# State-space layer: the product of the scores between two row tiles with weighted x as three fp32r passes over high and low parts instead of one plain fp32 matmul, with one buffer for the far sum

## The chip, the core and the metric

The kernel runs on one core of one Trainium2 chip. The metric is the device time of one execution in microseconds; the time quoted is the median of several runs. Besides the runs, one execution is profiled. TensorE (PE in the profile, with its weight loads as PEld), VectorE (DVE), ScalarE (ACT), GpSimd (POOL) and SyncE (SP, which here issues nearly all transfers) work from queues of their own and wait for each other through semaphores.

## The reference

A decoder trunk of two layers on 256 tokens of width 2048: an attention layer (MLA) and a state-space layer (SSM), each followed by a squared-ReLU MLP, all in fp32. What matters here is the scan of the SSM layer, which with 256 tokens is one chunk. It has 8 groups of 8 heads of 64 channels, and states of 128.

```
cum = jnp.cumsum(la_c, axis=1)
decay = jnp.exp(jnp.where(tril[None, :, :, None, None], diff, -jnp.inf))
cb = jnp.einsum('blgn,bsgn->blsg', c_c, b_c)
y_diag = jnp.einsum('blsgh,bsghp->blghp', cb[..., None] * decay, x_c)
```

So each head's output is a lower-triangular 256 by 256 matrix (scores `cb` times decay) times x.

## The kernel before

Tokens lie in two row tiles of 128. The triangle is cut into two tiles on the diagonal, which are computed head by head, and one full tile that leads from the first 128 tokens to the last 128. The decay in that tile splits into a factor of the source row and a factor of the target row. So the tile is done for a whole group at once: x of the first row tile is multiplied by the source factor (`edge[:, 0]`, on GpSimd, line 1257), the scores between the row tiles (`cb[g][:, P:256]`, 128x128) are multiplied with it on TensorE (128x512, line 1261), and VectorE multiplies the result by the target factor into `far[g]` (line 1263). GpSimd later adds `far[g]` to the second row tile (line 1314), and VectorE adds the diagonal products (line 1320).

Almost all of TensorE's work is large matrix products in fp32r. Every operand is held as a high part (rounded to fp32r by a ScalarE copy) and a low part (the rest, a VectorE subtraction), and a product is three passes: high times high, low times high, high times low. Weights arrive in units of 128x1024: SP loads one (`wraw`, line 85, six buffers), ScalarE writes its high part (`wh`, line 102), VectorE its low part (`wl`, line 103), four buffers each, and TensorE uses it in twelve matmuls of 512 columns (lines 339, 340, 343). The product of line 1261 is not of this kind: both operands are plain fp32.

A block is a set of four keys, each of two such units; after each key `tick()` runs what has been put off with `later(n, ...)`, so a step put off by 0 comes one tick later and one put off by 1 two ticks later. TensorE's order is the order in which the program is written. For the other engines a scheduler sets the order; `behind("last")`, `behind("last_lo")` and `behind("last_load")` put an instruction behind the last `wh` copy on ScalarE, the last `wl` subtraction on VectorE, or the last weight load on SP.

`x_block(g)` computes x of group g. Its convolution reads three shifted copies of x from DRAM (`taps`, two transfers of 768 KB, line 1229) and the convolution weights (`cw`, 128x2560, one buffer, line 1213), multiplies them (lines 1234 and 1235), sums them (1239) and applies SiLU (1244, 1247). Then `ahead` starts the heads of the group and the product described above. `head` loads a row of cumulative sums for each head (`cm`, line 1287) and builds the decay (ACT lines 1291 and 1292, DVE line 1294). Scratch tiles of 128x512 come from a pool of seven (`s2`).

Of the kernel before, what the change touches and what calls it, by code (L numbers as in the profile page):

```python
# [20 lines left out]
F32 = mybir.dt.float32  # L21
F32R = mybir.dt.float32r
I32 = mybir.dt.int32
AF = mybir.ActivationFunctionType
ALU = mybir.AluOpType
# [3 lines left out]
P = 128  # L29
# [185 lines left out]
class Trunk:  # L215
# [851 lines left out]
    def ssm_body(self, sp, dp, gain):  # L1067
        nc, d, cst = self.nc, self.d, self.cst
# [9 lines left out]
        cb = [None] * GROUPS  # L1078
# [4 lines left out]
        far = [None] * GROUPS  # L1083
# [18 lines left out]
        def behind(what):  # L1102
            return self.tc.issue_after(getattr(self.flow, what).ins)
# [88 lines left out]
        def cb_group(g):  # L1192
            B, C = fm["B", g // 4][:, g % 4], fm["C", g // 4][:, g % 4]
            b = self.bank(early[0])
            nc.tensor.matmul(b[:, 0:256], B[:, 0:P], C, start=True, stop=True)
            nc.tensor.matmul(b[:, 256:384], B[:, P:256], C[:, P:256], start=True, stop=True)
            t = sp.tile([P, 384], F32, tag="cb", name=f"cb{g}", bufs=5)
            for o in (0, 256):
                nc.vector.scalar_tensor_tensor(t[:, o:o + P], b[:, o:o + P], 0.125, tri[:, 0:P], ALU.mult, ALU.mult)
            cb[g] = t  # L1200

            def far_part():
                with behind("last"):
                    nc.scalar.activation(t[:, P:256], b[:, P:256], AF.Copy, scale=0.125)

            self.later(0, far_part)

        def x_block(g):
            cw = []

            def weights():
                cw.append(sp.tile([P, 2560], F32, tag="cw", name=f"cw{g}", bufs=1))
                nc.sync.dma_start(cw[0], d["cwx"][g])

            self.later(3, weights)
            accs = self.block([("si", "x", g, q) for q in range(4)], xT)
            xt = sp.tile([P, 2, 512], F32, tag="xtm", name=f"xtm{g}", bufs=3)
            x = [xt[:, t] for t in range(2)]
            th = [None, None]
            for t in range(2):  # L1220
                nc.scalar.activation(x[t], accs[t], AF.Copy, scale=rs[t])
            nc.scalar.dma_start(xD[3:S + 3, g * 512:g * 512 + 512].rearrange("(t p) n -> p t n", t=2), xt)

            def shift():
                with behind("last_load"):
                    for t in range(2):
                        v = xD[t * P:t * P + P, g * 512:g * 512 + 512]
                        row = v.ap[0][0]
                        nc.sync.dma_start(taps[:, t], bass.AP(tensor=v.tensor, offset=v.offset, ap=[[row, P], [row, 3], [1, 512]]))

            def mult(t):
                flat = taps[:, t].rearrange("p i n -> p (i n)")
                with behind("last_lo"):
                    nc.vector.tensor_tensor(flat, flat, cw[0][:, :1536], ALU.mult)
                    nc.vector.tensor_tensor(x[t], x[t], cw[0][:, 1536:2048], ALU.mult)

            def total(t):
                for v in (taps[:, t, 2], taps[:, t, 1], taps[:, t, 0], cw[0][:, 2048:]):
                    nc.vector.tensor_tensor(x[t], x[t], v, ALU.add)

            def tanh(t):
                th[t] = self.scratch()
                with behind("last"):
                    nc.scalar.activation(th[t], x[t], AF.Tanh, scale=0.5)

            def silu(t):
                nc.vector.scalar_tensor_tensor(x[t], th[t], 1.0, x[t], ALU.add, ALU.mult)

            def ahead():
                xg[g] = x  # L1250
                dg = self.gain_tile(d["dsk"][g])
                for i in range(8):
                    hq.append((g, i, dg))
                heads_of = lambda v: v.rearrange("p (h f) -> p h f", h=8)
                spread = lambda v: v[:, 8 * g:8 * g + 8].unsqueeze(2).to_broadcast([P, 8, 64])
                xw = self.scratch()
                nc.gpsimd.tensor_tensor(heads_of(xw), heads_of(x[0]), spread(edge[:, 0]), ALU.mult)

                def across():
                    b = self.bank(False)  # L1260
                    nc.tensor.matmul(b, cb[g][:, P:256], xw, start=True, stop=True)
                    far[g] = sp.tile([P, 512], F32, tag="far", name=f"far{g}", bufs=2)
                    nc.vector.tensor_tensor(heads_of(far[g]), heads_of(b), spread(edge[:, 1]), ALU.mult)

                self.later(1, across)

            self.later(2, shift)
            if g >= 4:
                self.later(2, lambda: cb_group(g))
            self.later(4, lambda: (mult(0), mult(1)))  # L1270
            self.later(5, lambda: total(0))
            self.later(6, lambda: (tanh(0), total(1)))
            self.later(7, lambda: (silu(0), tanh(1), silu(1), ahead()))

        def pump():
# [88 lines left out]
        for step in SSM_ORDER:  # L1364
            kind, i = step[0], int(step[1])
# [242 lines left out]
```

## Time and profile before

| | before |
|---|---|
| runs | 2285.92 us median of 3 (2285.37 to 2287.04) |
| the profiled execution | 2286.35 us, of which the span is 2284.5 |
| TensorE / VectorE / ScalarE / GpSimd busy | 100% / 84% / 61% / 12% of the span |
| granted TensorE clock | 1.00 |
| SSM groups' product (line 1261) | 8 of them, at 1080.5 to 1502.6 us of the span |

Times in the profile are counted from the start of the span. A group row gives the line, engine, operation and tiles, then the number of instructions, their busy time in us and the mean of one in ns, then the idle time before them. A row of a timeline gives the start, the duration from first start to last end, and a count of equal instructions that follow each other; a bracket at its end is idle time before it and what ended that. TensorE's matmuls overlap, so their pace is read from starts. A plain fp32 matmul is recorded as two.

### The profile page before, as it was taken

Reading aid. Unit: us, or ns where it says so; the run is one execution under the profiler, and the core shown is the slowest. Engines: PE = TensorE matmul, PEld = TensorE weight load, DVE = VectorE, ACT = ScalarE, POOL = GpSimd, SP = SyncE. Lnnn points to the kernel's source line nnn. Section 1 sums busy time; section 2 is a strip of 40 time slices with the busy share of each in tenths; the row PEclk is TensorE's granted clock in tenths of the full one; section 3 lists DMA queues with packets and bytes.
Section 4 is the critical chain, followed back from the end, with each engine's and each line's share of the span. In section 5 each row is a group of like instructions: output and inputs, shape, how many; then the busy total and the mean of one; then the engine's idle time right before and its main releaser. Section 6 shows DMA issues by size and latency. Waiting matters only on the chain.

```text
span 2284.5 us, 30768 instructions
## 1 busy us (share of the span) xinstructions
PE 2278.1 (100%) x10929; PEld 1889.6 (83%) x10929; DVE 1915.9 (84%) x2318; ACT 1390.1 (61%) x1947; POOL 275.5 (12%) x315
## 2 busy tenths in 40 slices
PE   9999999999999999999999999999999999999999
PEld 7898888888888888888888888888888888888887
DVE  7786698999898897687899688676989889989985
ACT  7775576566666666564666555545666666666663
POOL 1440000000000000100133213121000000000000
PEclk9999999999999999999999999999999999999999
DMA  8545678888888878667888787767688888888874
GB/s 315 173 153 159 211 230 267 259 255 270 264 255 259 267 232 271 227 208 241 277 280 278 245 275 264 229 222 229 204 265 248 259 270 253 260 275 247 267 232 160
DMA packets 167706, 557.16 MB, mean 244 GB/s; under 512 B 19040, under 2 KB 28192, under 8 KB 166528
## 3 DMA queue, kind: packets, MB, share of 16 engines
q1 hardware_dynamic: 151264, 502.44, 66.2%
q0 software_dynamic: 13888, 48.49, 10.0%
q10 hardware_dynamic: 2400, 4.27, 0.5%
q8 instruction: 86, 1.41, 0.3%
q14 instruction: 68, 0.56, 0.1%
HBM read 529.65 MB, written 6.41 MB: 235 GB/s over the span
## 4 chain that ended last, share of the span: by engine, by line
PE 96%; DVE 1%; DMA 1%; ACT 1%; issue 1%; POOL 0%; SPq 0%; ACTq 0%; DVEq 0%
PE acc L339 13%; PE acc L340 13%; PE acc L343 13%; PE yp L618 9%; PE yp L617 9%; PE yp L616 9%; PE st L617 7%; PE st L618 7%; PE st L616 7%; DMA wraw<-mi 1%; PE sm L324 1%; DVE wl L103 1%; PE y L1309 1%; PE sm L322 1%; PE acc L616 1%; PE acc L618 1%
## 5 line engine op out<-in xcount | busy, mean ns | idle before, releaser
L102 ACT ACTIVATE wh<-wraw 128x1024 fp32r<-128x1024 f32 (+1 forms) x818 | 856.2, 1053 | 570.4 <-PE acc L340 268.9
L103 DVE TENSOR_TENSOR wl<-wraw,wh 128x1024 fp32r<-128x1024 f32 (+1 forms) x818 | 985.5, 1221 | 240.6 <-ACT wh L102 216.6
L616 PE MATMUL yp<-wh,k 128*128 128x512 f32 x896 | 349.2, 390 | 0.0
L618 PE MATMUL yp<-wh,k 128*128 128x512 f32 x896 | 348.8, 389 | 0.0
L617 PE MATMUL yp<-wl,k 128*128 128x512 f32 x896 | 348.6, 389 | 0.0
L339 PE MATMUL acc<-wh,xt 128*128 128x512 f32 x704 | 279.7, 397 | 0.4 <-ACT wh L102 0.4
L340 PE MATMUL acc<-wh,xt 128*128 128x512 f32 x704 | 274.9, 390 | 0.1
L102 ACT ACTIVATE wh<-wrx 128x1024 fp32r<-128x1024 f32 x168 | 177.8, 1058 | 153.4 <-PE yp L618 101.7
L103 DVE TENSOR_TENSOR wl<-wrx,wh 128x1024 fp32r<-128x1024 f32 x168 | 204.3, 1221 | 36.6 <-ACT wh L102 35.6
L618 PEld LDWEIGHTS yp<-wh,k 128*128 128x128 f32 x896 | 168.2, 188 | 35.1
L617 PEld LDWEIGHTS yp<-wl,k 128*128 128x128 f32 x896 | 168.2, 188 | 34.9
L616 PEld LDWEIGHTS yp<-wh,k 128*128 128x128 f32 x896 | 168.2, 188 | 34.8
L339 PE MATMUL acc<-wh,k 128*128 128x512 f32 x496 | 196.5, 396 | 0.0
L340 PE MATMUL acc<-wh,k 128*128 128x512 f32 x496 | 193.3, 390 | 0.0
L343 PE MATMUL acc<-wl,xt 128*128 128x512 f32 x704 | 188.3, 389 | 0.0
L616 PE MATMUL st<-wh,xt 128*128 128x512 f32 x448 | 177.7, 397 | 0.0
L618 PE MATMUL st<-wh,xt 128*128 128x512 f32 x448 | 174.9, 390 | 0.0
L617 PE MATMUL st<-wl,xt 128*128 128x512 f32 x448 | 174.7, 390 | 0.0
L339 PEld LDWEIGHTS acc<-wh,xt 128*128 128x128 f32 x704 | 132.7, 188 | 29.4 <-ACT wh L102 1.6
L340 PEld LDWEIGHTS acc<-wh,xt 128*128 128x128 f32 x704 | 132.5, 188 | 28.5 <-issue 1.2
L343 PEld LDWEIGHTS acc<-wl,xt 128*128 128x128 f32 x704 | 132.1, 188 | 27.7
L199 POOL DMA_DIRECT2D wrx<-mi x56 | 49.2, 878 | 720.6 <-DVE wl L103 524.5
(318 smaller groups left out, 3527.0 us busy)
## 6 DMA issues: line engine op xcount, KB each, us to landing
wraw<-mi SPq DMA_DIRECT2D x256, 512.0 KB, 5.5
wraw<-mo SPq DMA_DIRECT2D x256, 512.0 KB, 5.6
wraw<-si SPq DMA_DIRECT2D x160, 512.0 KB, 5.2
wraw<-so SPq DMA_DIRECT2D x64, 512.0 KB, 5.2
wrx<-mi SPq DMA_DIRECT2D x56, 512.0 KB, 5.4
wrx<-mi POOLq DMA_DIRECT2D x56, 512.0 KB, 7.8
wraw<-wo SPq DMA_DIRECT2D x32, 512.0 KB, 4.0
taps<-xD SPq DMA_DIRECT2D x16, 768.0 KB, 8.4
```

Of the source, the lines that this page charges most:

```text
L102: self.last = nc.scalar.activation(h[:, v], raw[:, v], AF.Copy)
L103: self.last_lo = nc.vector.tensor_tensor(lo[:, v], raw[:, v], h[:, v].bitcast(F32), ALU.subtract)
L199: nc.gpsimd.dma_start(st["b11"].tile, quarter(d, 1, 0), accum_op=ALU.add)
L322: self.nc.tensor.transpose(b.bitcast(F32R)[:, v], words[:, v], self.ident_r)
L324: self.nc.tensor.transpose(b[:, v], src[:, v], self.ident)
L339: nc.tensor.matmul(accs[t][:, :n], ah, wh[:, q, :], start=first and kt + q == 0, stop=False)
L340: nc.tensor.matmul(accs[t][:, :n], al, wh[:, q, :], start=False, stop=False)
L343: nc.tensor.matmul(accs[t][:, :n], lhs(kt + q, t)[0], wl[:, q, :], start=False, stop=en and q == nk - 1)
L616: nc.tensor.matmul(b, ah, wh, start=first and q == 0, stop=False)
L617: nc.tensor.matmul(b, ah, wl, start=False, stop=False)
L618: nc.tensor.matmul(b, al, wh, start=False, stop=last and q == 1)
L1309: nc.tensor.matmul(y[t][c, o], part(t)[:, c], xg[g][t][:, o], start=True, stop=True)
```

## The change

```
-                xw = self.scratch()
+                xw = cw[0][:, :512]
+                xh, xl = (self.s2.tile([P, 512], F32R, tag="s2", name=self.name("xw")) for _ in range(2))
+                fh = sp.tile([P, 2, P], F32R, tag="fh", name=f"fh{g}", bufs=1)
                 nc.gpsimd.tensor_tensor(heads_of(xw), heads_of(x[0]), spread(edge[:, 0]), ALU.mult)
+                with behind("last"):
+                    nc.scalar.activation(fh[:, 0], cb[g][:, P:256], AF.Copy)
+                with behind("last_lo"):
+                    nc.vector.tensor_tensor(fh[:, 1], cb[g][:, P:256], fh[:, 0].bitcast(F32), ALU.subtract)
+
+                def parts():
+                    with behind("last"):
+                        nc.scalar.activation(xh, xw, AF.Copy)
+                    with behind("last_lo"):
+                        nc.vector.tensor_tensor(xl, xw, xh.bitcast(F32), ALU.subtract)
+
+                self.later(0, parts)
 
                 def across():
                     b = self.bank(False)
-                    nc.tensor.matmul(b, cb[g][:, P:256], xw, start=True, stop=True)
-                    far[g] = sp.tile([P, 512], F32, tag="far", name=f"far{g}", bufs=2)
+                    for i, (a, w) in enumerate(((0, xh), (0, xl), (1, xh))):
+                        nc.tensor.matmul(b, fh[:, a], w, start=i == 0, stop=i == 2)
+                    far[g] = sp.tile([P, 512], F32, tag="far", name=f"far{g}", bufs=1)
                     nc.vector.tensor_tensor(heads_of(far[g]), heads_of(b), spread(edge[:, 1]), ALU.mult)
 
                 self.later(1, across)
```

The scores (`fh`) and weighted x (`xh`, `xl`) are split like other operands, and the product becomes three fp32r passes. The scores are split in `ahead` itself, weighted x one tick later, and the passes come another tick later, at the product's place. Weighted x in fp32 has no scratch tile of its own any more: it overwrites the first 512 columns of the group's convolution weights. The new tiles `xh` and `xl` come from the pool of scratch tiles. `far` has one buffer instead of two. Lines behind the edit are 15 higher in the changed kernel: 1294 is 1309, 1320 is 1335, 1287 is 1302, and 1263 is 1278 there; its product is line 1276.

The order on VectorE around the product of group 2, before. `wl` are low parts of weights, `mt` the decays of single heads, `xtm` is x (the L1320 rows add the diagonal products of group 1):

```order
L103 TENSOR_TENSOR wl_10830<-wraw_10727,wh_10829 128x1024
L1320 SCALAR_TENSOR_TENSOR xtm_9865<-xtm_9865,y_0_10690 128x512
L1320 SCALAR_TENSOR_TENSOR xtm_9865<-xtm_9865,y_1_10691 128x512
L103 TENSOR_TENSOR wl_10866<-wraw_10745,wh_10865 128x1024
L1294 SCALAR_TENSOR_TENSOR mt_10995<-mt_10995,dt,cb_9591 128x128 x2
```

The same place in the changed kernel. The row of line 1269 writes `xl` (named `xw` here, as `xh` is) from weighted x in `cw`:

```order
L103 TENSOR_TENSOR wl_10850<-wraw_10743,wh_10849 128x1024
L1335 SCALAR_TENSOR_TENSOR xtm_9869<-xtm_9869,y_0_10706 128x512
L1335 SCALAR_TENSOR_TENSOR xtm_9869<-xtm_9869,y_1_10707 128x512
L1269 TENSOR_TENSOR xw_10786<-cw_10325,xw_10785 128x512
L103 TENSOR_TENSOR wl_10888<-wraw_10761,wh_10887 128x1024
L103 TENSOR_TENSOR wl_10906<-wraw_10829,wh_10905 128x1024
```

The subtraction stands behind the two adds and ahead of the low parts of the next weight units.

The order on SP's queue at the load of group 2's convolution weights (`cw`), before. `wraw` are weight units, `cm` cumulative sums of heads, `taps` the shifted copies of x of group 2:

```order
L1213 DMA cw_10313<-cwx 128x2560
L85 DMA wraw_10391<-si 128x1024
L85 DMA wraw_10409<-si 128x1024
L85 DMA wraw_10439<-si 128x1024
L1287 DMA cm_10795<-cumD 128x256
L1287 DMA cm_10847<-cumD 128x256
L85 DMA wraw_10457<-si 128x1024
L1229 DMA taps<-xD 128x3x512 x2
```

The same stretch in the changed kernel:

```order
L1302 DMA cm_10815<-cumD 128x256
L85 DMA wraw_10405<-si 128x1024
L85 DMA wraw_10423<-si 128x1024
L85 DMA wraw_10455<-si 128x1024
L1302 DMA cm_10869<-cumD 128x256
L1213 DMA cw_10325<-cwx 128x2560
L85 DMA wraw_10473<-si 128x1024
L1229 DMA taps<-xD 128x3x512 x2
```

The load of `cw`, which needs the buffer that now holds weighted x of group 1, stands three weight units and two `cm` rows later, with one weight unit between it and `taps`.

On TensorE only the product itself differs: one row of line 1261 is now three of line 1276 at the same place.

## The prediction

> **What bounds the kernel now.** I read the page first, then the waits of TensorE over the whole run, then the busy time of the engines in stretches of the SSM layer, then the timelines around each of the eight products that change.
>
> ```profile
> span 2284.5 us, 30768 instructions
> PE 2278.1 (100%) x10929; PEld 1889.6 (83%) x10929; DVE 1915.9 (84%) x2318; ACT 1390.1 (61%) x1947; POOL 275.5 (12%) x315
> PE 96%; DVE 1%; DMA 1%; ACT 1%; issue 1%; POOL 0%; SPq 0%; ACTq 0%; DVEq 0%
> ```
>
> TensorE is busy for the whole span and is 96% of the chain that ended last. Its waits for other engines, line by line (total, times, longest), in the whole run:
>
> ```profile
> PE warmed L451 <- DVE warm L448: 1.4, 1, 1.4
> PE yp L939 <- ACT xt L944: 0.5, 1, 0.5
> PE yp L939 <- DVE qn L887: 0.4, 1, 0.4
> PE acc L339 <- ACT wh L102: 0.4, 1, 0.4
> ```
>
> That is 2.7 us in all, none of it in the SSM layer. So nothing can be gained but TensorE's own work, and any new wait of TensorE is added in full. The engine that is nearest to causing one is VectorE. Two stretches of the SSM layer (busy time of TensorE, weight load, VectorE, ScalarE, GpSimd, then granted clock, DMA share and GB/s):
>
> ```profile
> 1122.00:1131.00 9.00, 9.00 (x39) 7.11 (x38) 9.00 (x15) 7.09 (x14) 1.43 (x1) 1.00 1.01 386
> 1144.50:1177.60 33.10, 33.10 (x205) 27.11 (x204) 32.48 (x43) 18.54 (x35) 15.37 (x8) 1.00 0.78 256
> ```
>
> VectorE has no idle time in the first and 0.62 us of 33.1 in the second. Its queue runs behind there, and what is newly put into it comes out late. The first row also shows the DMA engines full at 386 GB/s.
>
> **What the change takes from TensorE.** One product and its neighbours on TensorE, for group 2 (start, duration, a count at the end):
>
> ```profile
> 1174.57 1.07 PE L343 MATMUL acc<-wl,xt 128*128 128x512 f32 x4
> 1175.48 1.02 PE L1261 MATMUL sm<-s,cb 128*128 128x512 f32 x2
> 1175.93 0.80 PE L339 MATMUL acc<-wh,xt 128*128 128x512 f32 x1
> 1176.57 0.40 PE L340 MATMUL acc<-wh,xt 128*128 128x512 f32 x1
> ```
>
> Durations overlap, so I go by starts. Four fp32r products take 1175.48 - 1174.57 = 0.91, 0.23 us each. From the start of the plain fp32 product (one instruction, recorded twice) to that of L340 are 1.09 us, of which one slot of 0.23 is the L339 between: the product costs 0.86. Three fp32r passes cost 3 x 0.23 = 0.68. The saving is 0.18 us, times 8 groups 1.4 us. It is on the path.
>
> **What it adds to the other engines.** Nearest rows (count, busy total, mean ns) for the four splits per group:
>
> ```profile
> L1235 DVE TENSOR_TENSOR xtm<-xtm,cw 128x512 f32<-128x512 f32 x16 | 10.9, 680 | 0.0
> L1199 DVE SCALAR_TENSOR_TENSOR cb<-sm,tri 128x128 f32<-128x128 f32 x12 | 2.9, 283 | 0.0
> L1244 ACT ACTIVATE s<-xtm 128x512 f32<-128x512 f32 x16 | 9.8, 625 | 17.8 <-DVE xtm L1239 17.7
> L1204 ACT ACTIVATE cb<-sm 128x128 f32<-128x128 f32 x6 | 1.6, 262 | 0.3 <-DVE cb L1199 0.3
> ```
>
> The high parts cost ScalarE 0.63 + 0.26 us, the low parts VectorE 0.68 + 0.28, per group. ScalarE has room (18.54 of 33.10) and its share counts as nothing. VectorE's share matters for when the low part of weighted x (`xl`) is ready, since the second of the three passes needs it. It waits for the multiply on GpSimd, the copy on ScalarE, and whatever stands ahead of it in VectorE's queue. The product's place on TensorE is fixed, between the same two units of weights as before, so I can set the two times against each other. In the new order `xl` stands in groups 1, 2, 3, 4 and 6 right behind the two L1320 adds. In groups 0, 5 and 7 the queue is short. The row on VectorE (for group 0 on GpSimd) that goes before `xl` in the new order, and the product, group by group (group 2's product is above):
>
> ```profile
> 1075.29 3.64 POOL L1257 TENSOR_TENSOR s<-xtm,edge 128x512 f32<-128x512 f32 x1 [119.67 <-PE acc L343]
> 1080.47 1.02 PE L1261 MATMUL sm<-s,cb 128*128 128x512 f32 x2
> 1127.10 1.27 DVE L1320 SCALAR_TENSOR_TENSOR xtm<-xtm,y 128x512 f32<-128x512 f32 x2
> 1128.10 1.02 PE L1261 MATMUL sm<-s,cb 128*128 128x512 f32 x2
> 1175.23 1.27 DVE L1320 SCALAR_TENSOR_TENSOR xtm<-xtm,y 128x512 f32<-128x512 f32 x2
> 1222.61 1.27 DVE L1320 SCALAR_TENSOR_TENSOR xtm<-xtm,y 128x512 f32<-128x512 f32 x2
> 1222.86 1.02 PE L1261 MATMUL sm<-s,cb 128*128 128x512 f32 x2
> 1269.71 1.27 DVE L1320 SCALAR_TENSOR_TENSOR xtm<-xtm,y 128x512 f32<-128x512 f32 x2
> 1270.92 1.02 PE L1261 MATMUL sm<-s,cb 128*128 128x512 f32 x2
> 1358.46 0.35 DVE L1294 SCALAR_TENSOR_TENSOR mt<-mt,dt,cb 128x128 f32<-128x128 f32 x1
> 1362.50 1.02 PE L1261 MATMUL sm<-s,cb 128*128 128x512 f32 x2
> 1409.33 1.27 DVE L1320 SCALAR_TENSOR_TENSOR xtm<-xtm,y 128x512 f32<-128x512 f32 x2
> 1410.56 1.02 PE L1261 MATMUL sm<-s,cb 128*128 128x512 f32 x2
> 1497.82 1.94 DVE L103 TENSOR_TENSOR wl<-wraw,wh 128x1024 fp32r<-128x1024 f32 x1
> 1502.14 1.02 PE L1261 MATMUL sm<-s,cb 128*128 128x512 f32 x2
> ```
>
> `xl` ends at the end of that row plus 0.28 (the other subtraction, queued a little earlier) plus 0.68, less two overlaps of 0.08, so plus 0.80. TensorE wants it at the product's start plus the 0.23 of the first pass. Group 1: 1128.37 + 0.80 = 1129.17 against 1128.33, a wait of 0.84. Group 2: 1177.30 against 1175.71, 1.59. Group 3: 1224.68 against 1223.09, 1.59. Group 4: 1271.78 against 1271.15, 0.63. Group 6: 1411.40 against 1410.79, 0.61. Group 0: GpSimd ends at 1078.93, copy and subtraction bring it to 1080.24 against 1080.70, no wait. Groups 5 and 7: 1359.6 against 1362.73 and 1500.6 against 1502.37, no wait. The sum is 5.3 us. Behind a waiting TensorE stand only its own next matmuls, which are the path.
>
> **What moves on SP's queue.** The weighted x now lies in `cw`, the buffer of the convolution weights. The load of the next group's `cw` must therefore wait until `xl` is written, and stands three weight loads later, just ahead of the `taps` loads. Before, for group 2 on SP, with median landing times (us, last column) of these transfers, then what ScalarE and VectorE did once the loads were there:
>
> ```profile
> 1129.54 0.33 SPq L85 DMA_DIRECT2D wraw<-si  x1
> 1129.96 0.92 SPq L1229 DMA_DIRECT2D taps<-xD  x2
> 1130.97 0.72 SPq L85 DMA_DIRECT2D wraw<-si  x1
> wraw<-si SPq DMA_DIRECT2D x160, 512.0 KB, 5.2
> taps<-xD SPq DMA_DIRECT2D x16, 768.0 KB, 8.4
> cw<-cwx SPq DMA_DIRECT2D x8, 1280.0 KB, 7.6
> 1141.90 1.06 ACT L102 ACTIVATE wh<-wraw 128x1024 fp32r<-128x1024 f32 x1 [0.51 <-PE acc L340]
> 1144.47 2.84 DVE L1234 TENSOR_TENSOR taps<-taps,cw 128x1536 f32<-128x1536 f32 x1
> ```
>
> The wait on SP itself hides: `xl` of group 1 comes at 1129.2, and the weight load behind it went out at 1129.54 anyway. Transfer time does not hide as well. `cw` is 1280 KB, at 386 GB/s 3.4 us, and now stands in front of `taps` and the weights behind them. `taps` issued by 1130.9 land some 8.4 + 3.4 later, by 1142.7, still ahead of the multiply at 1144.47. The weights issued at 1130.97 were to land after 5.2 us and two `taps` of 768 KB (1573 KB in all, 4.1 us), near 1140.3; with 3.4 more near 1143.7. ScalarE wanted them at 1141.90, so its split, VectorE's split and the multiply behind come up to 1.8 us late. VectorE has but 0.62 us idle until group 2's adds at 1175.23, so most of that reaches group 2's `xl`, and TensorE. The same pattern follows for groups 3 and 4. For 5 and 7 other blocks lie between the two loads, and for 6 `cw` goes out early, since `xl` of group 5 comes at 1359.6. Bounds for these three: 0 each (TensorE has meanwhile been pushed back by earlier waits, and the loads catch up) and 3.4 each, 10.2 in all. I take 1.0 each, 3.0, between the 0 and the 1.8 worked out here.
>
> The cumulative-sum rows (`cm`) that now go out ahead of `cw` reach ScalarE earlier, which is not on the path. One buffer for the far sum makes its writer on VectorE wait for the GpSimd add (L1314) of the group before; that add stands in GpSimd's queue ahead of this group's multiply (L1257), which the product itself needs, so it is done by then and costs nothing.
>
> [...] The longest wait of TensorE in the rows above is 1.4 us, and the clock granted is 1.00 in both stretches. [...]
>
> **The sum.** The profiled execution took 2286.35 us, 1.85 more than its span and 0.43 more than the median 2285.92 of the runs. -1.4 + 5.3 + 3.0 = +6.9, or 2293.25 on the profiled time, and 2292.8 as a median, 0.30% slower. A measurement of this kernel can tell about 0.2%, 4.6 us, from no change: above 2290.5 is slower, below 2281.3 faster.
>
> **The rivals.**
> (a) The waits for `xl` come but the loads catch up: -1.4 + 5.3 = +3.9, 2289.8, within 0.2%. For it speaks that DMA share is 0.78 in the long stretch; against it that the queue is full just where `cw` now goes.
> (b) Nothing waits, and the change gives what its three passes save: 2284.5, not slower. Place: the second pass of each product. It decides at the point where `xl` ends before the product's start plus 0.23; in groups 0, 5 and 7 it does, in five others VectorE would have to be 0.6 to 1.6 us ahead of where its rows stand. The order gives it nothing to get ahead with.
> [...]
> (d) The plain fp32 product holds TensorE longer than its neighbours' starts show, so that three passes save over 4.6 us. That takes 0.58 us more in each, and the chain runs on without a gap behind it; I see no place for it.
>
> **How the numbers follow.** The forecast has 0.60, (a) 0.22, (b) 0.10, (c) 0.05, (d) 0.03. Slower is the forecast and (c), 0.65; the same is (a) and (b), 0.32; faster is (d), 0.03. The range's upper end is the sum with the full 10.2, 2300.0. The lower end is 2285.5, waits of 1.0 us in all against the 1.4 saved. It leaves out (b), (c) and (d), 0.18.
>
> **What would show it.** In the profile after: a line of TensorE's waits for VectorE at the new product, absent before, of 5 to 15 us over at least five groups, with the longest in groups 2 and 3 and none in 5 and 7; matmul spacing of 0.23 within the three passes; the multiply of `taps` in groups 2 to 4 later against TensorE. If the waits sum to under 2 us, my reading of VectorE's queue is wrong; if they sum to 5 and no more, the loads were covered; if TensorE waits at L339 or L343 instead, the late weights reach it directly.

## The result and the profile after

The changed kernel takes 2294.01 us (median of 7 runs, 2292.47 to 2294.68) where the kernel before takes 2285.92 (7 runs): ratio 1.0032, 95% interval 1.0022 to 1.0043. It is slower by 8.1 us by the medians, 7.3 by the ratio. The forecast was 2292.8. The profiled execution took 2294.01 us, its span is 2292.2.

The page of the changed kernel: span, busy time of the engines, and the shares of the chain that ended last.

```profile
span 2292.2 us, 30831 instructions
PE 2278.5 (99%) x10937; PEld 1890.6 (82%) x10937; DVE 1917.9 (84%) x2334; ACT 1396.3 (61%) x1963; POOL 274.5 (12%) x315
PE 88%; DVE 6%; DMA 2%; issue 2%; ACT 1%; POOL 0%; SPq 0%; DVEq 0%; ACTq 0%; POOLq 0%
```

TensorE is busy for as long as before (2278.5 against 2278.1 us), but the span is 7.7 us longer and VectorE's share of the chain has gone from 1% to 6%. TensorE's waits, by line (total, times, longest), say where:

```profile
PE sm L1276 <- DVE xw L1269: 6.8, 5, 2.0
PE warmed L451 <- DVE warm L448: 1.4, 1, 1.4
PE sm L322 <- DVE k L300: 0.6, 2, 0.4
```

The first line is new: five of the eight products wait for VectorE's low part of weighted x (`xl`, called `xw` in the rows). Durations of matmuls overlap (0.39 us each, started 0.23 apart), so this sum is a little short. By starts, the time from a product's first pass to the next L339, less the 0.68 of three passes, is 0, 1.63, 2.25, 1.99, 1.20, 0, 1.13 and 0 us for groups 0 to 7: 8.2 in all. Group 2 on TensorE, then the same moment on VectorE:

```profile
1177.60 0.39 PE L1276 MATMUL sm<-xw,fh 128*128 128x512 f32 x1
1179.96 0.73 PE L1276 MATMUL sm<-xw,fh 128*128 128x512 f32 x2 [1.98 <-DVE xw L1269]
1180.53 0.40 PE L339 MATMUL acc<-wh,xt 128*128 128x512 f32 x1
```

```profile
1176.89 1.22 DVE L103 TENSOR_TENSOR wl<-wraw,wh 128x1024 fp32r<-128x1024 f32 x1
1178.03 1.28 DVE L1335 SCALAR_TENSOR_TENSOR xtm<-xtm,y 128x512 f32<-128x512 f32 x2
1179.22 0.68 DVE L1269 TENSOR_TENSOR xw<-cw,xw 128x512 fp32r<-128x512 f32 x1
```

The first pass runs at 1177.60. `xl` stands behind the weight split and the two L1335 adds, with no idle time on VectorE, and ends at 1179.90. The second pass starts 0.06 later. The last two passes then take 0.57 us instead of 0.46.

The products of groups 0 and 7 on TensorE give the balance of everything between them:

```profile
1081.39 0.61 PE L1276 MATMUL sm<-xw,fh 128*128 128x512 f32 x2
1509.84 0.84 PE L1276 MATMUL sm<-xw,fh 128*128 128x512 f32 x3
```

They are 428.45 us apart; before, 1502.14 - 1080.47 = 421.67. That is 6.8 more: the 8.2 of waits less 1.6 that seven products save (measured below, in versions without the waits), to within 0.2. Another 0.9 of the difference of the two profiled executions was there before the first product (1081.39 against 1080.47). No step of the change accounts for it; in nine versions measured below that product starts anywhere from 1079.24 to 1080.78, so it is most likely scatter.

The load of `cw` on SP's queue (start, duration), then ScalarE and VectorE when the loads behind it are wanted:

```profile
1130.51 0.33 SPq L1213 DMA_DIRECT2D cw<-cwx  x1
1131.65 0.33 SPq L85 DMA_DIRECT2D wraw<-si  x1
1132.07 1.91 SPq L1229 DMA_DIRECT2D taps<-xD  x2
1145.88 1.06 ACT L102 ACTIVATE wh<-wraw 128x1024 fp32r<-128x1024 f32 x1 [2.37 <-DMA wraw<-si]
1148.12 1.75 DVE L1234 TENSOR_TENSOR taps<-taps,cw 128x1536 f32<-128x1536 f32 x1
```

The page's rows on both loads, with the median time to landing at the end:

```profile
taps<-xD SPq DMA_DIRECT2D x16, 768.0 KB, 10.0
cw<-cwx SPq DMA_DIRECT2D x8, 1280.0 KB, 8.1
```

The load goes out just ahead of `taps`, `taps` take 10.0 us to land and not 8.4, and ScalarE now stands still for 2.37 us until a weight unit has landed, where before it waited 0.51 for TensorE. `cw` itself is in time: by its median it lands near 1138.6, the multiply that reads it starts at 1148.12. That multiply starts 3.65 later than before (1144.47), while TensorE's product is 2.12 later (1177.60 against 1175.48). VectorE has caught up with some of it by then: it is busy for 32.88 of the 33.5 us that follow, as it was before.

```profile
1148.00:1181.50 33.50, 31.52 (x199) 25.82 (x198) 32.88 (x45) 22.71 (x45) 14.59 (x7) 1.00 0.78 250
```

So two things could cause the loss, and they meet in the same wait: the place of `xl` in VectorE's queue, and the late load of `cw`. The experiments take them apart.

### The profile page after: what moved, and what is told of

Same layout as the page of the kernel before. It is cut to its first block, busy times and chain, and to the rows that moved or that the text cites. A ratio compares the mean times of both kernels' runs of the same rounds, so it can differ in the third digit from the quotient of the medians.

```text
span 2292.2 us, 30831 instructions
## 1 busy us (share of the span) xinstructions
PE 2278.5 (99%) x10937; PEld 1890.6 (82%) x10937; DVE 1917.9 (84%) x2334; ACT 1396.3 (61%) x1963; POOL 274.5 (12%) x315
## 4 chain that ended last, share of the span: by engine, by line
PE 88%; DVE 6%; DMA 2%; issue 2%; ACT 1%; POOL 0%; SPq 0%; DVEq 0%; ACTq 0%; POOLq 0%
PE acc L339 12%; PE acc L340 12%; PE acc L343 12%; PE yp L617 8%; PE yp L618 8%; PE yp L616 8%; PE st L617 7%; PE st L618 7%; PE st L616 7%; DVE wl L103 3%; DMA wraw<-mi 2%; ACT wh L102 1%; PE sm L324 1%; PE acc L617 1%; PE acc L618 1%
## 5 line engine op out<-in xcount | busy, mean ns | idle before, releaser
L339 PE MATMUL acc<-wh,xt 128*128 128x512 f32 x704 | 277.7, 394 | 0.1
L339 PE MATMUL acc<-wh,k 128*128 128x512 f32 x496 | 195.3, 394 | 0.0
L343 PE MATMUL acc<-wl,xt 128*128 128x512 f32 x704 | 188.3, 389 | 0.0
L339 PEld LDWEIGHTS acc<-wh,xt 128*128 128x128 f32 x704 | 132.7, 189 | 28.0 <-ACT wh L102 0.6
L343 PEld LDWEIGHTS acc<-wl,xt 128*128 128x128 f32 x704 | 132.1, 188 | 27.7
```

Source lines behind the costliest of these rows:

```text
L339: nc.tensor.matmul(accs[t][:, :n], ah, wh[:, q, :], start=first and kt + q == 0, stop=False)
L343: nc.tensor.matmul(accs[t][:, :n], lhs(kt + q, t)[0], wl[:, q, :], start=False, stop=en and q == nk - 1)
```

## The experiments

My theory (T below): TensorE's waits for `xl` are the whole loss; most of it comes from the place of `xl` behind the adds, some 3 us from the late `cw` load. Rivals: the queue alone (R2), the late load alone or other late transfers (R1), the single buffer of the far sum (R3). All times below are medians; "against before" is against the kernel before on the same chip in the same comparison.

**Weighted x in a scratch tile of its own.** The load of `cw` is early again.

```
-                xw = cw[0][:, :512]
+                xw = self.scratch()
```

> Weighted x gets a scratch tile of its own again, and the load of cw its early place ahead of the three weight units; everything else is as changed, xl behind the L1335 adds too. If the waits have two causes (T: xl's place behind the adds some 5.3 us, the late cw load some 3.0), TensorE's waits at the new product fall from 8.2 us to about 5, the split of weights behind taps waits under 1 us for its load again, and the time is about 2291, some 3 us under the changed kernel's. If only VectorE's queue causes them (R2: cw's place costs nothing), waits stay near 8 and the time near 2294. If the cw load alone does (R1), they vanish and the time is about 2286.

Measured: 2290.83 us, +4.7 against before, ratio 1.0022 (1.0013 to 1.0031).

```profile
PE sm L1276 <- DVE xw L1269: 5.8, 5, 1.5
```

The waits stay in all five groups (by starts 1.01, 1.82, 1.82, 0.78 and 1.76 in groups 1, 2, 3, 4 and 6: 7.2 in all). About 3 of the 8 us are gone by the medians, so neither the queue alone nor the load alone fits. But the waits fell by 1.0 and not by 3, as my theory had it (group 6 has 1.76 where the changed kernel has 1.13), and the products of groups 0 and 7 are 427.52 us apart, only 0.9 less than in the changed kernel. What the late load is worth here is thus not settled by this run alone.

**The passes one tick later.** The `cw` load stays late.

```
-                self.later(1, across)
+                self.later(2, across)
```

> The three passes go one tick (two weight units, some 5.4 us) later; xl, the cw load and all splits stay where the change put them. T: the waits at the product are the whole cost, the longest is about 2 us, so 5.4 us cover all of them: no wait of TensorE at the product, and 8 to 9 us under the changed kernel, about 2285 (before less 1.4 for the three passes is 2284.5). If the added work on ScalarE and VectorE or the late loads hold TensorE up by themselves (R1), the waits come back at the weights (L339, L343) and the time stays above 2290.

Measured: 2291.60 us, +5.5, ratio 1.0022 (1.0013 to 1.0031); single runs from 2288.75, the profiled one, to 2293.92. My theory missed this by 6 to 7 us.

```profile
PE acc L343 <- DVE wl L103: 2.5, 3, 1.9
PE sm L322 <- DMA tr<-s: 0.5, 1, 0.5
```

The wait at the product is gone, as expected, and TensorE waits for the low parts of the weights (L343) instead. The way there runs through ScalarE: between 1040 and 1540 us its splits wait 11.8 us for weight units of this layer's input (`si`) to land, 6.2 in the changed kernel and not at all before. The late load does reach TensorE by itself.

**Both: own scratch tile and the later passes.** The edits of the two kernels above together.

> Both: weighted x in a scratch tile of its own, and the passes one tick later. T: no wait at the product and no late load, 2284.5, the saving of the three passes alone; equal to the version with the later passes only, within 1 us, since without a wait at the product the late load has nobody to delay. If the late load reaches TensorE in another way (R1), this one is some 3 us faster than the version with the later passes alone.

Measured: 2284.39 us, -1.75, ratio 0.9995 (0.9986 to 1.0003). It is 7 us under the version with the later passes alone, where my theory had both equal and R1 had 3. So the late load, with no wait at the product, costs 7 us; with that wait in the way it costs 3, by the medians. The profiled execution, at 2286.21 us one of the slowest of the eleven, has one wait at the weights:

```profile
PE acc L343 <- DVE wl L103: 1.1, 1, 1.1
```

**No low part of weighted x.** The late part of the queue's wait goes with it, since `cw` is free when the copy `xh` has been written.

```
-                    with behind("last_lo"):
-                        nc.vector.tensor_tensor(xl, xw, xh.bitcast(F32), ALU.subtract)
...
-                    for i, (a, w) in enumerate(((0, xh), (0, xl), (1, xh))):
+                    for i, (a, w) in enumerate(((0, xh), (0, xh), (1, xh))):
```

> Leaves out the low part of weighted x: xl is not computed, and the second pass multiplies the high part once more, so TensorE does the same three passes. T: what the product waits for is VectorE's xl alone; xh, which ScalarE writes, is early. So no wait at the product, and about 2284.5 to 2286. If the cw load costs by itself (R1), the load waits for xh in place of xl and still stands behind the three weight units: some of the 3 us should stay, 2288 or so, with waits at other lines.

Measured: 2284.55 us, -1.6, ratio 0.9995 (0.9986 to 1.0004). TensorE has no wait at the product and none at the weights in the SSM layer. The load on SP's queue, for group 2:

```profile
1125.09 0.33 SPq L1213 DMA_DIRECT2D cw<-cwx  x1
1126.49 2.66 SPq L85 DMA_DIRECT2D wraw<-si  x2
1129.25 1.08 SPq L1229 DMA_DIRECT2D taps<-xD  x2
```

It goes out 4.2 us ahead of `taps` instead of 1.6, with two weight units between, and costs nothing. VectorE has one subtraction per group less to do here, so the run does not test sharing alone; it suggests that sharing is harmless as such, and that what costs is how late `xl` frees the buffer.

**The pass with `xl` last.**

```
-                    for i, (a, w) in enumerate(((0, xh), (0, xl), (1, xh))):
+                    for i, (a, w) in enumerate(((0, xh), (1, xh), (0, xl))):
```

> Order of the three passes: high x high, low scores x high, then high x low, so xl is wanted one pass (0.23 us) later. T: each of the five waits is 0.23 shorter, 1.1 us in all, waits of 7.0 and a time of about 2293. If the passes waited for the low part of the scores (R), or for something that is not xl, nothing changes, 2294.

Measured: 2292.62 us, +6.3, ratio 1.0030 (1.0019 to 1.0041): not to be told from the changed kernel. In the trace the third pass waits, not the second (group 2: the first two at 1176.56, the third at 1179.50 after 2.33 us), so it is `xl` that is waited for. The time is near the 2293 expected, but the waits by starts sum to 8.0 and not to 7.0: three are shorter, those of groups 1 and 2 longer than in the changed kernel. After the longest, in group 2, TensorE's clock is down. Windows (busy times, then granted clock, DMA share, GB/s):

```profile
1180.00:1182.00 2.00, 2.00 (x8) 1.54 (x7) 2.00 (x4) 0.00 (x0) 0.00 (x0) 0.70 0.96 264
1182.00:1184.00 2.00, 2.00 (x6) 1.60 (x5) 2.00 (x5) 1.06 (x1) 0.00 (x0) 0.50 0.96 317
1184.00:1186.00 2.00, 2.00 (x9) 1.59 (x9) 2.00 (x4) 0.00 (x0) 0.00 (x0) 0.95 0.93 342
```

**The kernel before with weighted x in `cw` only.** Plain fp32 product.

```
-                xw = self.scratch()
+                xw = cw[0][:, :512]
```

> The kernel before with one part of the change only: weighted x lies in the cw buffer, so that the load of the next cw waits for the product itself. Plain fp32 product, no splits. T: the cw load comes late and the splits behind taps with it, but TensorE waits for nothing of VectorE at the product, so hardly anything shows: 2286 to 2288. If a late load costs by itself (R1), 3 us or more: 2289 and above, with waits of TensorE at the weights.

Measured: 2292.64 us, +6.3, ratio 1.0027 (1.0017 to 1.0038). Again my theory missed and R1 held. There is no `xl` here, and TensorE waits at the weights:

```profile
PE acc L343 <- DVE wl L103: 4.3, 4, 2.4
```

The load goes out at 1130.48 for group 2, between the two `taps` and not ahead of both, so it is not quite the late load of the changed kernel. After the wait of 2.4 us the clock is at 0.68, 0.50 and 0.97 in the next three stretches of 2 us: another 1.7 us lost.

**The kernel before with one buffer for the far sum only.**

```
-                    far[g] = sp.tile([P, 512], F32, tag="far", name=f"far{g}", bufs=2)
+                    far[g] = sp.tile([P, 512], F32, tag="far", name=f"far{g}", bufs=1)
```

> The kernel before with one part of the change only: one buffer for the far sum in place of two. T: GpSimd's add of the group before stands ahead of what the product needs, so nothing waits: 2286, no difference within 0.5 us. If the buffer costs (R3), VectorE waits at the far sum and the time is 1 us or more above.

Measured: 2286.80 us, +0.5, ratio 1.0002 (0.9993 to 1.0010). No difference, and the products of groups 0 and 7 are 421.68 us apart, as before (421.67); R3 falls.

**The splits at once.** `xl` ahead of the adds on VectorE, `cw` shared.

```
-                self.later(0, parts)
+                parts()
```

> The two splits of weighted x are issued at once behind its multiply, not one tick later: xl stands ahead of the L1335 adds in VectorE's queue, and VectorE may have to wait there for GpSimd's multiply (3.64 us) and the copy on ScalarE. T: xl is ready before the product and its waits go, below 2 us in all; what VectorE idles in front of xl (up to some 4 us a group) it may owe to the weight splits behind it: 2285 to 2291. If the place behind the adds is not the cause (R1), waits stay near 8 and the time at 2294.

Measured: 2298.09 us, +11.7, ratio 1.0046 (1.0032 to 1.0060), the slowest of all, and outside what I expected.

```profile
PE acc L343 <- DVE wl L103: 4.3, 2, 2.2
PE acc L339 <- ACT wh L102: 2.3, 2, 1.6
PE acc L340 <- DVE k L300: 1.9, 1, 1.9
```

The wait at the product is gone and stands at the weights instead (of the two at L339 only the one of 1.6 us; the other lies at the start of the program). After three of these waits, 2.17 us twice and 1.93, the clock is at one half. VectorE now stands idle in front of `xl`:

```profile
DVE xw L1269 <- ACT xw L1267: 5.9, 5, 1.6
```

In the changed kernel that line has 1.6 us in one group.

**The same with a scratch tile of its own.** Both edits, to see which part of that is the late load.

> Weighted x in a scratch tile of its own, passes at their place, and the two splits issued at once behind the multiply. With the shared tile that took 2298.1, TensorE waiting at the weights and its clock at 0.50 for about 3 us after three of these waits. If the late cw load made those waits: none of them here, and 2284.5 to 2287. If VectorE and ScalarE stand idle in front of the splits and give that back at the weights: 2290 or more, TensorE waiting for wh and wl.

Measured: 2291.57 us, +5.5, ratio 1.0024 (1.0014 to 1.0034).

```profile
PE acc L343 <- DVE wl L103: 2.2, 2, 1.7
PE acc L340 <- DVE k L300: 1.3, 1, 1.3
PE acc L339 <- ACT wh L102: 1.0, 2, 0.6
```

With the load early, the waits at the weights remain in part (of the row on L339 only 0.4 us lies in this layer), and the clock stays up in the profiled execution. So moving `xl` forward on VectorE only moves the debt from the product to the weight splits behind it. The other 6 us go with the late load and the falls of the clock, three of 1.7 us in the profiled execution.

**The convolution weights in two tiles.** Only the last 512 columns (256 KB) are shared with weighted x; the 1024 KB for `taps` load early.

```
-                cw.append(sp.tile([P, 2560], F32, tag="cw", name=f"cw{g}", bufs=1))
-                nc.sync.dma_start(cw[0], d["cwx"][g])
+                cw.append(sp.tile([P, 2048], F32, tag="cw", name=f"cw{g}", bufs=1))
+                nc.sync.dma_start(cw[0], d["cwx"][g][:, :2048])
+
+            def bias():
+                cw.append(sp.tile([P, 512], F32, tag="cb512", name=f"cwb{g}", bufs=1))
+                nc.sync.dma_start(cw[1], d["cwx"][g][:, 2048:])
...
+            self.later(3, bias)
...
-                xw = cw[0][:, :512]
+                xw = cw[1]
```

> The changed kernel with the convolution weights in two tiles: taps' 2048 columns (1024 KB) in one that is free as early as before, the 512 columns of the last term (256 KB) in a second one, and weighted x shares the second only. The passes stay at their place. If the lateness of 1280 KB just ahead of taps is worth the 3.2 us between the changed kernel and the one with a scratch tile of its own, 256 KB late should cost a fifth of it or nothing: about 2291, waits of 5.5 to 7 at the product. If it is the wait for xl itself on SP's queue, ahead of taps, that costs and not the bytes, it stays near 2294.

Measured: 2291.59 us, +5.5, ratio 1.0024 (1.0014 to 1.0034). The waits by starts are 1.01, 1.82, 1.83, 0.80 and 0.77 in groups 1, 2, 3, 4 and 6, 6.2 in all, 2.0 less than in the changed kernel.

**Two tiles and the later passes.**

> The same two tiles, and the passes one tick later. With the one shared tile that version took 2291.6, with a scratch tile of its own 2284.4. If the bytes of the late load cause these 7 us: about 2284.5 to 2286, TensorE's waits at the weights under 2 us. If the queue's wait for xl causes them: about 2291.

Measured: 2284.71 us, -1.4, ratio 0.9994 (0.9986 to 1.0003). The small load still waits for `xl` just ahead of `taps`; the median landing time of `taps` is back at 8.4, and TensorE waits for nothing at the product or the weights of the SSM layer; ScalarE's splits wait 0.2 us for `si` units to land between 1040 and 1540 us, where with the whole tile late they waited 11.8. The row on `taps`, then the loads of group 2 and the products of groups 0 and 7 in the timeline, and TensorE's one wait between these products:

```profile
taps<-xD SPq DMA_DIRECT2D x16, 768.0 KB, 8.4
```

```profile
1128.78 0.33 SPq L1217 DMA_DIRECT2D cwb<-cwx  x1
1130.34 1.56 SPq L1234 DMA_DIRECT2D taps<-xD  x2
1085.71 0.61 PE L1281 MATMUL sm<-xw,fh 128*128 128x512 f32 x2
1506.19 0.62 PE L1281 MATMUL sm<-xw,fh 128*128 128x512 f32 x2
```

```profile
PE sm L322 <- DMA tr<-s: 0.2, 1, 0.2
```

It is thus the bytes ahead of `taps` and the weights, not SP's wait for `xl`: 1024 KB less there take away 6.9 us. `xl` of group 1 ends at 1128.76 here and the load goes out at 1128.78, so the wait on the queue is still there.

The products are 420.48 us apart; before, 421.67. Six of the seven steps from one product to the next are 0.22 or 0.23 shorter than before; the last, with the wait at L322, is 0.16 longer. In the version without the low part, which also runs three passes, all seven are 0.22 or 0.23 shorter, 1.6 in all (420.09). That is what the three passes save.

**`xl` on GpSimd.** Own scratch tile, passes at the place where the change put them.

```
-                xw = cw[0][:, :512]
+                xw = self.scratch()
...
-                        nc.vector.tensor_tensor(xl, xw, xh.bitcast(F32), ALU.subtract)
+                        nc.gpsimd.tensor_tensor(xl, xw, xh.bitcast(F32), ALU.subtract)
```

> Weighted x in a scratch tile of its own, the passes at their place, and xl subtracted by GpSimd, right behind its multiply, not by VectorE behind the adds (only VectorE's form of it took 2290.8). GpSimd's 128x512 rows take 1.5 to 1.9 us, so group 2's xl would be there near 1174.5, ahead of the second pass at 1175.1. If VectorE's queue is what the passes wait for: no waits at the product beyond 0.5 us a group, and about 2284.5 to 2286. If two splits of weighted x in time for the place are too much for any engine: 2289 or more, with waits for GpSimd.

Measured: 2286.40 us, +0.3, ratio 1.0003 (0.9994 to 1.0011). TensorE's one recorded wait at the product:

```profile
PE sm L1276 <- POOL xw L1269: 0.4, 1, 0.4
```

Group 2 on GpSimd and TensorE:

```profile
1170.70 2.57 POOL L1269 TENSOR_TENSOR xw<-s,xw 128x512 fp32r<-128x512 f32 x1 [0.92 <-ACT xw L1267]
1175.41 0.84 PE L1276 MATMUL sm<-xw,fh 128*128 128x512 f32 x3
```

GpSimd takes 2.57 us, longer than the 1.5 to 1.9 I had, and is still done at 1173.27, 2.4 us ahead of the second pass. The three passes run without a gap. Against VectorE's form (+4.7) 4.4 us are gone, with the product at the same place: what it waits for is VectorE's queue. The waits left (0.64 and 0.39 by starts, groups 0 and 1) take back more than half of the saving; the 0.64 is over the 0.5 I had as a limit, and the time just above the range I expected.

Put together, against before: no late load and no wait for `xl`, -1.4 to -1.75; the wait for `xl` alone, +4.7; the late load alone, +5.5 with the three passes and +6.3 with the plain product; both, +8.1. The two costs do not add: against the versions without either, the wait alone is 6.1 to 6.4 us, the late load alone 6.9 to 7.2, and both together are 9.5 to 9.8, not 13. The best two versions that compute all of it (the later passes with a scratch tile of its own, or with two tiles) are over 9 us under the changed kernel. Against the kernel before, the interval of either includes no change, so a gain of some 1.5 us is likely but not settled.

These are sums of medians, and a part of them is probably the clock. Over a whole run the mean granted clock is 0.999 in the two profiled executions with one fall of it and 0.998 in the one with three. Of all runs, it is 0.999 in four of the seven of the changed kernel, in seven of the ten with the later passes alone, and in four of the eight with the splits at once and an own scratch tile. It is 1.000 in all eleven of the first experiment and in all twenty with two tiles.

The profiled executions of the changed kernel, the first experiment, the later passes and the version without the low part have no such fall. In them the products of groups 0 and 7 are 420.09 us apart with neither cost (no low part), 427.52 with the wait alone (own scratch tile), 425.05 with the late load alone (later passes) and 428.45 with both. That is 7.4, 5.0 and 8.4 us. So the late load alone is smaller than by the medians, and the two do not add here either. Falls of the clock in the other runs would explain the rest, but one run of the splits at once shows 1.000 at 2298.08 us, so this stays open.

## Why the prediction was right, and where its terms were off

**The bound and the saving.** TensorE's waits were next to nothing before, and each new one counted in full: 8.2 of waits less 1.6 saved is, to within 0.2, the 6.8 between the products of groups 0 and 7. The saving of 0.18 per product was measured as 0.22 to 0.23, 1.8 in all and not 1.4. The working stopped one matmul behind the product, but the next ones are a little slower too: before, seven slots behind it take 1.62 us (1081.56 to 1083.18), in the changed kernel 1.58 (1082.30 to 1083.88).

**The waits for `xl`, 5.3.** The five groups named wait, the other three don't. Where the load is early (two tiles), they are 1.01, 1.82, 1.83, 0.80 and 0.77, against 0.84, 1.59, 1.59, 0.63 and 0.61: 6.2. Each is 0.16 to 0.24 longer. The step left out 0.17 of that: 0.06 from the end of `xl` to the second pass, and 0.11 because the third pass follows the second at 0.34 us after a wait, not at 0.23. I had put that spacing at 0.23 throughout, which holds only in groups that don't wait.

**The late load, +1.0 in each of groups 2, 3 and 4.** The multiply came late as foreseen and ScalarE waited for its weights 2.37 us in group 2, where I had up to 1.8. The part of it that reached the product, changed kernel against two tiles, is 0.62, 0.43, 0.16, 0.40 and 0.36 in groups 1, 2, 3, 4 and 6: 2.0 by these two executions, and by the medians 2.6 (3.4 against the version with a scratch tile of its own). So the sum was about right, but it is spread over five groups; groups 1 and 6, to which I gave none, have half of it. My waits came to 8.3 against 8.2 measured because, in these executions, the first term was 0.9 too small and the second 1.0 too large. That the sum is so close is luck: the mechanism is the one forecast, the two errors cancel.

**What was wrong with the reason given.** The price of the late load was right only beside the waits for `xl`. The prediction named as its lower bound that TensorE has been pushed back by earlier waits; the runs show that this is most of the matter. Without those waits the same load costs 6 to 7 us by the medians (5.0 in the profiled execution), through TensorE's waits at L343 for low parts of weights. The prediction looked for such waits only as the sign of its own failure, and the theory for the experiments dropped them; the three expectations that rested on it (later passes, both edits together, the plain product in `cw`) failed.

**The rivals.** (a), in which the loads catch up, is out: the time is above 2290.5, and giving the load its early place is worth 2.6 to 3.4 us by the medians (0.9 to 1.9 between the products of the profiled executions). (b) is what the kernel does once neither cause is there. (d) is out, as the saving shows. (c), given 0.05, is TensorE at half its rate after long waits; what it adds for that was the author's estimate, and no run shows that term. In the profiled execution of the changed kernel the clock is 1.00 after waits up to 1.98. In three of the other versions it fell to 0.50 after waits of 1.93 to 2.44, at 1.7 us a time, and the 0.999 in four runs of the changed kernel suggests that it fell there too. GpSimd's order covers the single far buffer, as said.

## What to carry to other kernels

When TensorE is the bound and never waits, splitting an operand for faster passes is worth only what the passes save (here 0.22 to 0.23 us a product), and the split has to be finished by an engine whose queue is short at that place (with `xl` on GpSimd, 4.4 of the 4.7 us were gone); compare the end of the row ahead of the split with the start of the pass that wants it. Before a tile is shared to save room, ask who writes it last, when that frees it, and what the next load then stands in front of: count the bytes ahead of the next urgent load, and share only the part that can be late (here 1024 KB less took away 6.9 us). Two delays that end in one wait need not add up: here they cost 6.1 to 6.4 and 6.9 to 7.2 us alone and 9.5 to 9.8 together. Each hid part of the other, so removing one returned less (2.6 to 3.4 us for the late load) than it costs alone.

## What the runs showed of the hardware

The granted clock fell to 0.50 after some waits of TensorE of about 2 us and stayed at 1.00 after others. In the version with the splits at once (`cw` shared), a wait of TensorE in the timeline:

```profile
1508.13 0.50 PE L340 MATMUL acc<-wh,k 128*128 128x512 f32 x1 [1.93 <-DVE k L300]
```

The windows after it (busy times, then granted clock, DMA share and GB/s):

```profile
1508.00:1510.00 2.00, 1.87 (x6) 1.33 (x7) 2.00 (x5) 1.80 (x2) 0.65 (x1) 0.85 0.17 70
1510.00:1512.00 2.00, 2.00 (x6) 1.56 (x5) 2.00 (x2) 0.82 (x2) 2.00 (x2) 0.50 0.04 8
1512.00:1514.00 2.00, 2.00 (x8) 1.60 (x8) 2.00 (x3) 1.12 (x3) 0.85 (x1) 0.79 0.52 135
```

A wait of 1.93 us was followed by a granted clock of 0.50; so were waits of 2.17 (twice), 2.33 and 2.44 us in these runs. Each lost 1.7 us by the windows (here 0.30 + 1.00 + 0.42), which makes 3.4 us at half rate. Waits of 1.98 us in the changed kernel and 1.88 in the version with the later passes were followed by 1.00. So some 2 us were enough in these runs, and 1.93 against 1.98 shows that the length alone doesn't decide; what does is not settled by them.
